# Layer 1's ConvFFN: seven block products for eight in the up-projection, and the down-projection as a stage of its own

## The chip, the core and the metric

The kernel runs on one core of a Trainium2 chip. The metric is the device time of one execution, in microseconds (us): before, 2966.02 as the median of three runs, which lie between 2965.62 and 2966.78.

## The reference

A backbone of two layers over 1024 latent tokens and 256 context tokens of width 1024, in float32. Layer 0 mixes tokens by latent attention and pooling, layer 1 by grouped-query attention; each layer ends with a ConvFFN on the modulated norm of the tokens, and the program with a norm. What this case touches is layer 1's second half and the final norm:

```python
def modulate(x, shift, scale):
    return rms_norm(x) * (1.0 + scale) + shift

def conv_ffn(h, w_up, conv_w, conv_b, w_down):
    a = h @ w_up                       # 1024 -> 2 x 2816
    g, u = a[..., :D_FF], a[..., D_FF:]
    # acc = conv_b + a convolution of width 3 over the tokens of g
    return (jax.nn.silu(acc) * u) @ w_down

xl = xl + ml[:, 2] * ol                # the attention's output
xl = xl + ml[:, 5] * conv_ffn(modulate(xl, ml[:, 3], ml[:, 4]), ...)
return rms_norm(xl, g_final)
```

## The kernel before, in words

Features lie on partitions and tokens along the free axis: a tile is 128 features x 512 tokens, and the 1024 latent tokens are two chunks (0 and 1). TensorE (PE) multiplies a 128x128 weight block with such a tile. To keep float32's accuracy each operand is split into a high and a low part (names in `h` and `l`), and `mm3` makes three matmuls of each product: high x high, high x low, low x high. A weight of 128x1024 is loaded by `wload` into one of two buffers `raw`; GpSimd (POOL, line 117) or ScalarE (ACT) makes the high part `wh`, and VectorE (DVE, line 111) subtracts it for the low part `wl`.

The 2816 features of the FFN are 22 tiles f. For each f of layer 1 `ffn` does the gate and the up-product of both chunks (4 x 24 matmuls: 8 blocks along the width of 1024, 3 matmuls each), the convolution (`conv`: ACT line 1645, DVE 1646 and 1647, ACT 1648) and the mix with u (`mix`: DVE 1656, ACT 1658, DVE 1659), which leaves the split activations `ah`, `al`. After every odd f, `product` adds the down-projection of two f's to the eight tiles of the stream x (2 x 8 x 6 matmuls, and 16 updates on DVE, line 1669).

`start1` writes the work around the FFN's beginning in the order in which each engine does it: the last out-projection's jobs (`out1`), with them the sum of squares and modulation of chunk 0 (`Norm`, `modulate1`), the first products of f = 0 on chunk 0, the norm of chunk 1, and then `n1.quick()`, the modulation of chunk 1's eight k-tiles (DVE lines 236, 249 and 251, POOL 238 and 239, a copy on ACT for each). `ahead(0)`, the gate of f = 1 on chunk 0, is what PE does meanwhile, and `gate(1, n1.QUICK)` takes chunk 1's k-tiles in the order in which they come.

Inside a region of `manual_schedule` the engines keep the code's order; code outside of one is put in order by a scheduler, each instruction where its engine is expected to be free. The FFN between `start1` and `finish1` is left to the scheduler. `finish1` is written out again: the tokens end in three pieces p, q and t (`Piece`: the last products, the update, squares, their sum over partitions on PE, the root by logarithm and exponential on ACT, lines 167 to 170, and the scaled output). ACT needs a table in its engine for these two functions; `tables` loads one ahead of its use (line 263).

## Time and profile before

| | before |
|---|---|
| runs, median of 3 | 2966.02 us |
| profiled execution, its span | 2965.5 us |
| PE busy | 2885.9 us (97%) |
| DVE busy | 1938.7 us (65%) |
| ACT busy | 1103.3 us (37%) |
| POOL busy | 741.1 us (25%) |
| matmuls | 15134 |
| layer 1's FFN begins (first gate product behind the out-projection) | 2208.84 us |
| its last full down-projection | 2914.64 us |

The profile covers one execution, from its first to its last instruction; what lies around the span is the half microsecond by which the runs' median is above it. A busy share is a mean over the whole program; what an engine means for the end is read from a stage: there one engine is busy all the time, or some wait ends last. The views used below are the windows (busy time of each engine in a stretch, the clock granted to PE, DMA), the chain of waits (followed back from the last instruction), groups of instructions by line, the timeline of single instructions, and the DMA issues.

### The profile page before, as it was taken

The page shows a single profiled execution, that of the slowest core. Times are in us where ns is not written, and L with a number is a line of the kernel's source. Part 1 is how long each engine was busy: PE and PEld are TensorE (multiplying, and loading weights), DVE is VectorE, ACT ScalarE, POOL GpSimd, SP SyncE. Part 2 cuts the span into 40 slices and gives each one's busy share as a digit, 9 for nine tenths or more (in the row PEclk, how much of TensorE's full clock was granted, in tenths as well). Part 3 has the DMA queues.
Part 4 walks back from the last instruction along what each step waited for, and adds up shares of the span by engine and source line. Part 5 has one row for each costly group of instructions (what it writes and reads, how often), then busy time and mean ns, then how long its engine had stood idle before and what let it go on. Part 6 is the DMA issues. An engine that isn't in the chain of part 4 may idle for free.

```text
span 2965.5 us, 39212 instructions
## 1 busy us (share of the span) xinstructions
PE 2885.9 (97%) x15134; PEld 2405.5 (81%) x15134; DVE 1938.7 (65%) x3268; ACT 1103.3 (37%) x2263; POOL 741.1 (25%) x858
## 2 busy tenths in 40 slices
...
GB/s 223 69 154 120 23 18 53 128 192 72 93 85 92 87 100 100 86 43 36 29 43 57 22 43 15 1 1 1 43 93 50 47 53 50 44 50 43 43 57 57
DMA packets 65971, 194.04 MB, mean 65 GB/s; under 512 B 8436, under 2 KB 13748, under 8 KB 65528
## 3 DMA queue, kind: packets, MB, share of 16 engines
...
q14 instruction: 68, 0.56, 0.1%
...
## 4 chain that ended last, share of the span: by engine, by line
PE 79%; DVE 11%; ACT 3%; issue 3%; POOL 2%; DMA 2%; SPq 0%; DVEq 0%; ACTq 0%; POOLq 0%
PE u L72 18%; PE g L72 18%; PE d L72 17%; PE b L72 6%; PE pv L1253 5%; PE T L1240 4%; PE S L1173 2%; PE S L1175 2%; PE S L1174 2%; PE qk L72 1%; PE T L72 1%; DVE h L249 1%; DVE mx L1196 1%; DVE y L236 1%; DVE wl L111 1%
## 5 line engine op out<-in xcount | busy, mean ns | idle before, releaser
L72 PE MATMUL g<-h,wh 128*128 128x512 f32 (+1 forms) x1760 | 507.0, 373 | 2.2 <-DVE h L249 2.2
L72 PE MATMUL u<-h,wh 128*128 128x512 f32 (+1 forms) x1760 | 505.3, 372 | 0.0
L117 POOL TENSOR_SCALAR wh<-raw 128x1024 fp32r<-128x1024 f32 x134 | 146.6, 1095 | 1086.3 <-PE d L72 428.9
L72 PEld LDWEIGHTS g<-h,wh 128*128 128x128 f32 x1760 | 319.2, 189 | 65.3 <-DVE h L249 3.8
L72 PEld LDWEIGHTS u<-h,wh 128*128 128x128 f32 x1760 | 319.2, 188 | 62.4
L1634 ACT COPY g<-g 128x512 f32<-128x512 f32 (+1 forms) x109 | 59.5, 546 | 788.5 <-PE g L72 788.5
L1669 DVE SCALAR_TENSOR_TENSOR x<-d,mod,x 128x512 f32<-128x512 f32 (+1 forms) x352 | 254.9, 735 | 147.6 <-PE d L72 146.9
L72 PE MATMUL g<-h,wl 128*128 128x512 f32 (+1 forms) x880 | 328.1, 373 | 2.5 <-DVE wl L111 2.5
L72 PE MATMUL u<-h,wl 128*128 128x512 f32 (+1 forms) x880 | 327.5, 372 | 0.2 <-DVE wl L111 0.2
L72 PE MATMUL d<-ah,wl 128*128 128x512 f32 (+1 forms) x832 | 308.3, 371 | 0.0
L72 PE MATMUL d<-al,wh 128*128 128x512 f32 (+1 forms) x832 | 307.7, 370 | 0.0
L72 PE MATMUL d<-ah,wh 128*128 128x512 f32 (+1 forms) x832 | 307.6, 370 | 0.0
L111 DVE TENSOR_TENSOR wl<-raw,wh 128x1024 fp32r<-128x1024 f32 x174 | 218.9, 1259 | 103.6 <-POOL wh L117 73.5
L1243 DVE TENSOR_TENSOR tl<-T,th 128x512 fp32r<-128x512 f32 x328 | 225.4, 687 | 46.7 <-ACT th L1242 41.6
L1253 PE MATMUL pv<-th,v 128*128 128x256 f32 x976 | 253.7, 309 | 1.4 <-ACT vo L1382 1.0
L1222 POOL TENSOR_SCALAR p<-p,sm 128x1280 f32<-128x1280 f32 x128 | 171.4, 1339 | 286.7 <-DVE sm L1221 194.3
L1196 DVE TENSOR_REDUCE mx<-S 128x1 f32<-128x512 f32 (+1 forms) x400 | 233.5, 584 | 10.9 <-PE S L1175 3.8
L1242 ACT CAST th<-T 128x512 fp32r<-128x512 f32 x328 | 192.3, 586 | 83.4 <-PE T L1240 75.2
L72 PE MATMUL b<-h,wh 128*128 128x512 f32 (+1 forms) x752 | 206.6, 362 | 4.6 <-DVE h L465 3.6
L1240 PE MATMUL T<-ident,p 128*128 128x128 f32 x1280 | 193.1, 272 | 1.5 <-POOL p L1222 1.5
L72 PEld LDWEIGHTS g<-h,wl 128*128 128x128 f32 x880 | 166.1, 189 | 33.8 <-DVE wl L111 3.0
L72 PEld LDWEIGHTS u<-h,wl 128*128 128x128 f32 x880 | 165.7, 188 | 31.7 <-DVE wl L111 0.6
...
## 6 DMA issues: line engine op xcount, KB each, us to landing
raw<-in_wup SPq DMA_DIRECT2D x88, 512.0 KB, 3.2
wm<-in_wmod SPq DMA_DIRECT2D x72, 512.0 KB, 3.6
raw<-in_wdn SPq DMA_DIRECT2D x44, 512.0 KB, 3.3
raw<-in_wout SPq DMA_DIRECT2D x32, 512.0 KB, 3.3
raw<-in_win SPq DMA_DIRECT2D x20, 512.0 KB, 3.8
wn<-in_wmodn SPq DMA_DIRECT2D x32, 256.0 KB, 5.3
xin<-in_xl SPq DMA_DIRECT2D x16, 256.0 KB, 6.0
wn<-in_wmodg SPq DMA_DIRECT2D x8, 512.0 KB, 3.9
```

What stands on the lines that cost most here:

```text
L72: PE.matmul(out, w, x, start=first and i == 0, stop=last and i == n - 1)
L111: eng.tensor_sub(lo[:, :n], raw[:, :n], f32(hi[:, :n]))
L117: P.tensor_scalar(out=hi[:, :n], in0=raw[:, :n], scalar1=1.0, scalar2=0.0, op0=ALU.mult, op1=ALU.add)
L1173: PE.matmul(o, qh, kh[:, ks], start=True, stop=False)
L1196: V.reduce_max(mx[:, j : j + 1], s, axis=AX.X)
L1222: P.tensor_scalar(out=self.p, in0=self.p, scalar1=sm[:, 3:4], scalar2=1.0, op0=ALU.mult, op1=ALU.mult)
L1240: PE.transpose(tb[:, (2 * j + i) * 128 : (2 * j + i) * 128 + 128], rows[i].p[:, c : c + 128], ident)
L1242: S.copy(hi, tb)
L1243: V.tensor_sub(lo, tb, f32(hi))
L1253: PE.matmul(out[0], st, mv, start=(u + j == 0 and x == 0), stop=(u + j == n - 1 and x == len(ops) - 1))
L1634: S.copy(g[:, G0[c] : G0[c] + n], b)
L1669: V.scalar_tensor_tensor(out=x, in0=b, scalar=mod[l, c // 2][:, 40 + d : 41 + d], in1=x, op0=ALU.mult, op1=ALU.add)
```

## The change

Four things change.

1. The up-projection of f = 1 to 21 is done as a product of 2x2 blocks: the width is cut in two halves of four k-tiles, the tokens in the two chunks, and the outputs in gate and up. In place of eight block products (of 12 matmuls each) there are seven (`strassen`, numbers 1 to 7), with sums and differences of the operands ahead and of the products behind. The weights' combinations are s1 to s4 (`wsum`, on POOL), a11 to a22 being the blocks themselves; each that is multiplied is split anew. The tokens' combinations t1 to t4 are made once, in the place of x (`Parts`). The products are added up in three PSUM banks x, y and z per f, and read by `u2`, `u3`, `c11`, `c12`, `c21` and `c22` of class `F`. f = 0 stays as it was.
2. The modulation is made in the place of x (`modulate_kept`), x itself having been stored in DRAM (`spill`) and being read back later.
3. The activations of each f are stored in DRAM (`store`), unsplit, and the down-projection follows as a stage of its own: `down(f)` loads weights and activations and splits both.
4. `finish1` becomes code behind that stage, with the same pieces in the same order; its `tables` call now follows code that is left to the scheduler.

```diff
+    def modulate_kept(k, x, r, m, first, dst, pool=True):
+        even = k % 2 == 0 or not pool
+        hi, lo = dst
+        sh = m[:, first * 8 + k : first * 8 + k + 1]
+        sc = m[:, first * 8 + 8 + k : first * 8 + 9 + k]
+        def scale():
+            if even:
+                V.scalar_tensor_tensor(out=x, in0=x, scalar=sc, in1=r, op0=ALU.mult, op1=ALU.mult)
+            else:
+                P.tensor_mul(x, x, r)
+                P.tensor_scalar(out=x, in0=x, scalar1=sc, scalar2=sh, op0=ALU.mult, op1=ALU.add)
+        def high():
+            if even:
+                S.activation(hi, x, AF.Identity, bias=sh)
+                S.activation(x, x, AF.Identity, bias=sh)
+            else:
+                S.copy(hi, x)
+        def low():
+            V.tensor_sub(lo, x, f32(hi))
+        return scale, high, low
...
+            if self.kept:
+                return modulate_kept(k, xs_of(self.c)[k], self.r, self.m, self.first, H[self.c][k], pool)
             return modulate1(k, xs_of(self.c)[k], self.r, self.n, self.m, self.first, tmp, H[self.c][k], pool, tag)
...
-        gate(0, range(6, 8))
-        load_ahead()
-        n1.total()
-        up(0, 1)
-        n1.root()
-        upper(0)
-        n1.rest()
-        up(1, 0)
-        load(1, 1)
-        n1.quick()
-        ahead(0)
-        gate(1, n1.QUICK)
-        mix(0)
-        upper(1)
-        down()
-        up(1, 1)
...
-    def finish1(gate, upper, conv, mix, down, product, spare):
-        regions.append(tc.manual_schedule(engines=ENGINES | {mybir.EngineType.SP}))
-        regions[-1].__enter__()
-        down()
...
-    ffn(1, (0, 1), (), start1, finish1)
+    d_act = tc.dram_tile([NF, 128, NLAT], F32, name="d_act")
...
+    def spill(d, c):
+        dma.dma_start(d_x[d][:, half_of(c)], xl[d][:, half_of(c)])
...
+    class Parts:
+        def __init__(self, j):
+            self.j = j
+            (self.b11, self.b12), (self.b21, self.b22) = [[xl[k][:, half_of(c)] for c in (0, 1)] for k in (j, j + 4)]
+        def first(self, e3, e1, e2):
+            e3.tensor_sub(self.b22, self.b22, self.b12)
+            e1.tensor_sub(self.b12, self.b12, self.b11)
+            e2.tensor_add(self.b11, self.b22, self.b11)
+        def fourth(self, eng):
+            eng.tensor_sub(self.b21, self.b21, self.b11)
...
+    def load_u(f, s):
+        rawu[f, s] = wpool.tile([128, 1024], F32, name="raw", tag="raw", bufs=2)
+        dma.dma_start(rawu[f, s], a["wup"][1, 2 * f + s])
...
+    SUMS = {"s1": ("a21", "a22", ALU.add), "s2": ("s1", "a11", ALU.subtract), "s3": ("a11", "a21", ALU.subtract), "s4": ("a12", "s2", ALU.subtract)}
+    def wsum(f, n, eng=P):
+        x, y, op = SUMS[n]
+        t = sums[f, n] = sp.tile([128, 512], F32, name="st", tag="st", bufs=3)
+        eng.tensor_tensor(out=t, in0=src_of(f, x), in1=src_of(f, y), op=op)
...
+    def wlow(f, n, eng=V):
+        hi, lo = A7[f, n]
+        eng.tensor_sub(lo, src_of(f, n), f32(hi))
...
+    PROD = {1: ("a11", "b11", "x"), 2: ("a12", "b21", "x"), 6: ("s2", "t2", "y"), 7: ("s3", "t3", "y"), 4: ("a22", "t4", "y"), 5: ("s1", "t1", "z"), 3: ("s4", "b22", "z")}
...
+    def strassen(f, i):
+        w, b, z = PROD[i]
+        if i in FIRST:
+            bank[f, z] = psb(z)
+        mm3(bank[f, z], [(wk(A7[f, w], j), operand_of(b, j)) for j in range(4)], first=i in FIRST, more=i not in FIRST)
...
+        def c22(self):
+            o = self.su[:, 512:1024]
+            V.tensor_add(o, bank[self.f, "z"], o)
+        def c12(self):
+            V.tensor_add(self.g_of(1), bank[self.f, "z"], self.u)
...
+        def store(self):
+            dma.dma_start(d_act[self.f], self.su[:, :1024])
...
+    b10 = plain(0, 1, 0, w0[1])
+    n1.rest()
+    for n in ("a11", "a12"):
+        whigh(1, n, P)
+    f0, f1 = F(0), F(1)
+    f0.open()
+    f1.open()
+    S.copy(f0.g_of(0), b00)
+    n1.quick()
+    wlow(1, "a11")
+    strassen(1, 1)
+    b01 = plain(0, 0, 1, w0[0], n1.QUICK)
+    wlow(1, "a12")
+    f1.s1()
...
+    for j, p in enumerate(parts):
+        p.first(P, V, V)
+        p.high(2, big() if j < 2 else small(spare[2 * j - 4]))
+        p.high(1, big() if j < 2 else small(spare[2 * j - 3]))
+        p.low(2)
+        p.low(1)
+    S.copy(f0.g_of(1), b01)
+    b11 = plain(0, 1, 1, w0[1])
+    strassen(1, 2)
...
+    def early(f):
+        me, old = fs[f], fs[f - 1]
+        nxt = f + 1 if f < NF - 1 else None
+        me.open()
+        strassen(f, 6)
+        old.c21()
+        whigh(f, "a22")
+        wlow(f, "a22")
+        if nxt:
+            load_u(nxt, 1)
+        old.conv(0)
+        strassen(f, 5)
+        me.u2()
+        old.conv2(0)
+        old.conv(1)
+        strassen(f, 2)
+        old.conv2(1)
+        old.silu(0)
+        old.mix(0)
+        if nxt:
+            whigh(nxt, "a11", P)
+        strassen(f, 7)
+        me.c11()
+        old.silu(1)
+        if nxt:
+            wlow(nxt, "a11")
+        old.mix(1)
+        old.store()
+    load_u(2, 0)
+    load_u(2, 1)
+    whigh(2, "a11", P)
+    wlow(2, "a11")
...
+    for f in range(1, NF):
+        nxt = f + 1 if f < NF - 1 else None
+        me, old = fs[f], fs[f - 1] if f > 1 else None
+        if f > 1:
+            early(f)
+        if nxt:
+            fs[nxt] = F(nxt)
+            strassen(nxt, 1)
+        me.u3()
+        me.c22()
+        if nxt:
+            wsum(nxt, "s1")
+            wsum(nxt, "s2")
+            whigh(nxt, "a12", P)
+            whigh(nxt, "s1")
+            whigh(nxt, "s2")
+        strassen(f, 3)
+        if nxt:
+            fs[nxt].s1()
+            wlow(nxt, "s2")
+            wlow(nxt, "s1")
+            wlow(nxt, "a12")
+            wsum(nxt, "s3")
+            whigh(nxt, "s3")
+        strassen(f, 4)
+        me.c12()
+        if nxt:
+            wlow(nxt, "s3")
+            wsum(nxt, "s4")
+            whigh(nxt, "s4")
+            wlow(nxt, "s4")
+            if nxt + 1 < NF:
+                load_u(nxt + 1, 0)
...
+    def down(f):
+        W[f] = wload(a["wdn"][1, f], p=dp if f % 4 > 1 else None, tag="dn" if f % 4 > 1 else "w")()
+        raw = wpool.tile([128, 1024], F32, name="raw", tag="raw", bufs=2)
+        dma.dma_start(raw, d_act[f])
+        acts[f] = {}
+        for c in (0, 1):
+            hi, lo = acts[f][c] = half("h"), half("h")
+            S.copy(hi, raw[:, half_of(c)])
+            V.tensor_sub(lo, raw[:, half_of(c)], f32(hi))
+    down(0)
+    down(1)
+    for f in range(0, NF - 2, 2):
+        down(f + 2)
+        down(f + 3)
+        for c in (0, 1) if f < NF - 4 else (0,):
+            for d in range(8):
+                product(c, d, 0, 512, (f, f + 1))()
+    regions.append(tc.manual_schedule(engines=ENGINES | {mybir.EngineType.SP}))
+    regions[-1].__enter__()
+    tables("natural_log_exp_and_others", False)
```

How this moves instructions is shown at three places, first the start of the FFN. On PE before, where the up-product of f = 0 ends; g is the gate of f = 1 on chunk 0 (`ahead`):

```order
L72 MATMUL u<-h,wh 128x512 x2
L72 MATMUL u<-h,wl 128x512
L72 MATMUL g<-h,wh 128x512 [waits Pool_49]
L72 MATMUL g<-h,wh 128x512
L72 MATMUL g<-h,wl 128x512 [waits DVE_49]
L72 MATMUL g<-h,wh 128x512 x2
L72 MATMUL g<-h,wl 128x512
L72 MATMUL g<-h,wh 128x512 x2
L72 MATMUL g<-h,wl 128x512
```

The same place on PE after; p is the plain product of f = 0, x the bank of block product 1 of f = 1, with the weight block a11:

```order
L72 MATMUL p<-h,wh 128x512 x2
L72 MATMUL p<-h,wl 128x512
L72 MATMUL x<-h,a11h 128x512 [waits Pool_49]
L72 MATMUL x<-h,a11h 128x512
L72 MATMUL x<-h,a11l 128x512 [waits DVE_49]
L72 MATMUL x<-h,a11h 128x512 x2
L72 MATMUL x<-h,a11l 128x512
L72 MATMUL x<-h,a11h 128x512 x2
L72 MATMUL x<-h,a11l 128x512
L72 MATMUL x<-h,a11h 128x512 x2
L72 MATMUL x<-h,a11l 128x512
L72 MATMUL p<-h,wh 128x512 [waits Activation_49]
```

24 matmuls on operands that only need a weight's low part have become 12, which wait for a11l. On DVE before, the end of chunk 1's modulation (lines 236 to 251) and what follows it:

```order
L236 SCALAR_TENSOR_TENSOR y<-x_6977,mod_66,r 128x512 [waits DVE_49]
L249 SCALAR_TENSOR_TENSOR h<-y,mod_66,h 128x512 [waits Activation_49]
L236 SCALAR_TENSOR_TENSOR y<-x_6979,mod_66,r 128x512 [waits DVE_49]
L249 SCALAR_TENSOR_TENSOR h<-y,mod_66,h 128x512 [waits Activation_49] x2
L251 TENSOR_TENSOR h<-z,h 128x512 [waits Activation_49]
L1646 SCALAR_TENSOR_TENSOR t_21647<-g,convw,t 128x512 [waits Activation_49]
L1647 SCALAR_TENSOR_TENSOR t<-g,convw,t_21647 128x512 [waits DVE_49]
L1656 TENSOR_TENSOR s<-t_21647,u 128x512 [waits PE_49,Activation_49]
L1659 TENSOR_TENSOR al<-s,ah 128x512 [waits Activation_49]
L111 TENSOR_TENSOR wl<-raw,wh 128x1024 [waits DMAHW3_49,Pool_49]
```

And after, where the modulation's low parts have line 277; x_6972 and the next are tiles of the stream, whose combinations (2471, 2472) and low parts (2486) come next:

```order
L264 SCALAR_TENSOR_TENSOR x_6979<-x_6979,mod_66,r 128x512 [waits DMAHW1_49]
L277 TENSOR_TENSOR h<-x_6977,h 128x512 [waits Activation_49]
L277 TENSOR_TENSOR h<-x_6979,h 128x512 [waits Activation_49]
L277 TENSOR_TENSOR h<-x_6975,h 128x512 [waits Activation_49]
L2524 TENSOR_TENSOR a11l<-raw,a11h 128x512 [waits DMAHW7_49]
L2524 TENSOR_TENSOR a12l<-raw,a12h 128x512
L2471 TENSOR_TENSOR x_6972<-x_6972 128x512 [waits Pool_49]
L2472 TENSOR_TENSOR x_6972<-x_6976,x_6972 128x512 [waits DVE_49]
L2486 TENSOR_TENSOR h<-x_6972,h 128x512 [waits Activation_49] x2
L2471 TENSOR_TENSOR x_6973<-x_6973 128x512 [waits Pool_49]
L2472 TENSOR_TENSOR x_6973<-x_6977,x_6973 128x512 [waits DVE_49]
```

The low part a11l, for which product 1 waits, stands behind the last of the modulation, and the convolution of f = 0 has moved behind the combinations.

The second place is the passage to the down-projection, which has none before. On PE after, in the last f: y takes block product 7 (weights s3), d is the first down product, z is product 3 (weights s4):

```order
L72 MATMUL y<-x_21787,s3h 128x512 x2
L72 MATMUL y<-x_21787,s3l 128x512
L72 MATMUL d<-h,wh 128x512 [waits Activation_49,Pool_49]
L72 MATMUL d<-h,wh 128x512 [waits DVE_49]
L72 MATMUL d<-h,wl 128x512
L72 MATMUL d<-h,wh 128x512 [waits Activation_49,Pool_49]
L72 MATMUL d<-h,wh 128x512 x2
L72 MATMUL d<-h,wl 128x512
L72 MATMUL d<-h,wh 128x512 [waits DVE_49]
L72 MATMUL d<-h,wl 128x512
L72 MATMUL d<-h,wh 128x512
L72 MATMUL z<-h,s4h 128x512 [waits DVE_49]
```

Six matmuls of the down-projection, which need the split weights and activations of f = 0 and 1, stand between block products 7 and 3 of the last f. What DVE does there, after; `h<-raw` at line 2815 is the low part of an activation read back, `su<-z` at 2568 is `c22`:

```order
L2583 SCALAR_TENSOR_TENSOR r<-g,convw,r 128x512 [waits Activation_49]
L2815 TENSOR_TENSOR h<-raw,h 128x512 [waits DMAHW4_49,Activation_49]
L2584 SCALAR_TENSOR_TENSOR r<-g,convw,r 128x512 [waits DVE_49]
L2815 TENSOR_TENSOR h<-raw,h 128x512 [waits Activation_49]
L111 TENSOR_TENSOR wl<-raw,wh 128x1024 [waits DMAHW5_49,Pool_49]
L2564 TENSOR_TENSOR su<-y,su 128x512 [waits DMAHW2_49,PE_49]
L2815 TENSOR_TENSOR h<-raw,h 128x512 [waits DMAHW6_49,Activation_49]
L2568 TENSOR_TENSOR su<-z,su 128x512 [waits DVE_49]
L2815 TENSOR_TENSOR h<-raw,h 128x512 [waits Activation_49]
L2829 SCALAR_TENSOR_TENSOR x_24940<-d,mod_66,x_24940 128x512 [waits DMAHW1_49,PE_49]
```

The weight low and the activations' lows of the down-projection stand among the convolution and the additions of the last f, two of them ahead of `c22` or just behind it.

The third place is on ACT. Before, the finish of the FFN: the table is loaded once, behind the last cast of the activations (the squares have line 2496):

```order
L1648 ACTIVATE t_25931<-t,convw 128x512 [waits DVE_49]
L1658 CAST ah<-s 128x512 [waits DVE_49]
L263 ACT_TABLE_LOAD
L2496 ACTIVATE x<-x_6972 128x512 [waits DVE_49]
L2496 ACTIVATE sq<-x_6973 128x512 [waits DVE_49,Pool_49]
L2496 ACTIVATE y<-x_6974 128x512 [waits DVE_49]
```

After, the first root of the finish; before these lines the same three activations stand without loads between them:

```order
L2862 ACTIVATE sq<-x_24942 128x256 [waits DVE_49,Activation_49]
L167 ACTIVATE x<-ss,epst 128x512 [waits PE_49]
L169 ACT_TABLE_LOAD
L169 ACTIVATE y<-x 128x512 [waits Activation_49]
L170 ACT_TABLE_LOAD
L170 ACTIVATE r<-y 128x512 [waits Activation_49]
L2862 ACTIVATE sq<-x_24934 128x256 [waits DVE_49]
```

And after, the start of the program, where before one load stands ahead of `scol`:

```order
L289 ACT_TABLE_LOAD x2
L514 ACT_TABLE_LOAD
L514 ACTIVATE scol<-scol 128x16 [waits DMAHW0_49]
L515 ACTIVATE srow<-srow 2x1024 [waits DMAHW1_49]
L289 ACT_TABLE_LOAD
```

A load now stands ahead of each logarithm (169) and each exponential (170) in the finish, in all three pieces, and the one of `tables` has moved to the start of the program.

## Rows read from the trace of the kernel before

**Rows 1.** Two lines of the profile's page: busy time of the engines, share of the span and instructions; and the DMA rate in the span's 40 equal slices.

```profile
PE 2885.9 (97%) x15134; PEld 2405.5 (81%) x15134; DVE 1938.7 (65%) x3268; ACT 1103.3 (37%) x2263; POOL 741.1 (25%) x858
...
GB/s 223 69 154 120 23 18 53 128 192 72 93 85 92 87 100 100 86 43 36 29 43 57 22 43 15 1 1 1 43 93 50 47 53 50 44 50 43 43 57 57
```

**Rows 2.** Windows: the stretch, its length, busy time and instructions of PE, PEld, DVE, ACT and POOL in it, the clock granted to PE, the DMA share and GB/s. The first is the start of layer 1's FFN, the second lies inside it, the last two are the finish.

```profile
2208.84:2256.84 48.00, 46.14 (x195) 36.11 (x195) 36.08 (x42) 19.97 (x30) 13.39 (x13) 1.00 0.23 77
2300.00:2850.00 550.00, 550.00 (x2370) 445.58 (x2369) 249.01 (x312) 89.11 (x134) 55.81 (x85) 1.00 0.14 48
2914.64:2949.40 34.76, 34.61 (x245) 32.10 (x243) 29.80 (x51) 20.07 (x38) 11.13 (x9) 1.00 0.15 54
2949.40:2965.50 16.10, 1.31 (x5) 0.64 (x3) 9.42 (x17) 6.04 (x15) 7.26 (x9) 0.57 0.43 147
```

**Rows 3.** Two links of the chain of waits in the steady FFN: start, duration, engine, output and line, instructions.

```profile
2256.84 22.29 PE d L72 x96
2279.13 11.16 PE g L72 x48
```

**Rows 4.** Timeline at the FFN's start: start, duration, engine, line, operation, out<-in, instructions. PE's first two matmuls behind the up-product of f = 0, then DVE's first and last step of chunk 1's modulation.

```profile
2220.92 0.63 PE L72 MATMUL g<-h,wh 128*128 128x512 f32 x2
...
2220.35 2.46 DVE L236 SCALAR_TENSOR_TENSOR y<-x,mod,r 128x512 f32<-128x512 f32 x2
...
2232.90 0.68 DVE L251 TENSOR_TENSOR h<-z,h 128x512 fp32r<-128x512 f32 x1
```

**Rows 5.** Timeline of DVE and POOL in chunk 0's modulation, and two of DVE's steps later; in brackets the idle time ahead and what ended it.

```profile
2192.08 0.75 DVE L1354 SCALAR_TENSOR_TENSOR x<-b,mod,x 128x512 f32<-128x512 f32 x1 [0.92 <-PE b L72]
2192.75 1.19 DVE L236 SCALAR_TENSOR_TENSOR hi<-x,mod,r 128x512 f32<-128x512 f32 x1
2193.86 2.31 DVE L111 TENSOR_TENSOR wl<-raw,wh 128x1024 fp32r<-128x1024 f32 x1
...
2205.91 0.69 DVE L251 TENSOR_TENSOR h<-z,h 128x512 fp32r<-128x512 f32 x1 [5.35 <-PE b L72]
2206.52 0.68 DVE L1483 TENSOR_TENSOR x<-x,y 128x512 f32<-128x512 f32 x1
...
2191.23 1.29 POOL L238 TENSOR_TENSOR z<-x,r 128x512 f32<-128x512 f32 x1 [3.03 <-DVE h L251]
...
2193.37 1.73 POOL L1483 TENSOR_TENSOR x<-x,y 128x512 f32<-128x512 f32 x1
...
2201.01 1.30 POOL L1483 TENSOR_TENSOR x<-x,y 128x512 f32<-128x512 f32 x1
...
2213.81 0.69 DVE L1496 TENSOR_TENSOR lo<-x,hi 128x512 fp32r<-128x512 f32 x1 [0.69 <-ACT hi L1495]
...
2223.85 0.75 DVE L236 SCALAR_TENSOR_TENSOR y<-x,mod,r 128x512 f32<-128x512 f32 x1
```

**Rows 6.** Groups of instructions by line and shape from 2256 to 2900 us: count | busy us, mean ns of one | idle time ahead and what ended most of it.

```profile
L1669 DVE SCALAR_TENSOR_TENSOR x<-d,mod,x 128x512 f32<-128x512 f32 x152 | 112.9, 749 | 77.5 <-PE d L72 76.9
L111 DVE TENSOR_TENSOR wl<-raw,wh 128x1024 fp32r<-128x1024 f32 x57 | 69.5, 1219 | 39.5 <-POOL wh L117 39.3
L117 POOL TENSOR_SCALAR wh<-raw 128x1024 fp32r<-128x1024 f32 x57 | 59.9, 1050 | 404.9 <-PE d L72 183.8 <-issue 153.6 <-DMA raw<-in_wdn 23.7
...
L1658 ACT CAST ah<-s 128x512 fp32r<-128x512 f32 x37 | 23.0, 621 | 98.5 <-DVE s L1656 98.5
...
L1570 POOL TENSOR_SCALAR h<-raw 128x512 fp32r<-128x512 f32 x4 | 2.4, 620 | 9.4 <-DMA raw<-in_wdn 9.4
```

**Rows 7.** DMA issues of the page: count, KB each, median us from issue to landing. The first are the down-projection's weights, the second modulation weights at the program's start.

```profile
raw<-in_wdn SPq DMA_DIRECT2D x44, 512.0 KB, 3.3
...
wn<-in_wmodn SPq DMA_DIRECT2D x32, 256.0 KB, 5.3
```

**Rows 8.** Windows of 2 us early in the program, columns as in rows 2: PE has little to do in the first two.

```profile
60.00:62.00 2.00, 0.66 (x3) 0.19 (x1) 1.69 (x4) 1.27 (x2) 0.00 (x0) 1.00 0.00 0
62.00:64.00 2.00, 0.63 (x2) 0.31 (x2) 1.32 (x3) 0.62 (x1) 0.00 (x0) 0.98 0.00 0
64.00:66.00 2.00, 1.94 (x4) 1.12 (x5) 2.00 (x6) 1.27 (x2) 0.07 (x1) 0.50 0.00 0
66.00:68.00 2.00, 2.00 (x7) 1.58 (x7) 1.97 (x5) 1.57 (x4) 2.00 (x2) 0.67 0.00 0
```

**Rows 9.** Timeline of ACT in the finish (the table load between a cast and the first square, then logarithm and exponential of the first root), and of PE at the program's start.

```profile
2915.47 0.62 ACT L1658 CAST ah<-s 128x512 fp32r<-128x512 f32 x1 [1.14 <-DVE s L1656]
2916.11 1.28 ACT L263 ACT_TABLE_LOAD   x1
2917.51 0.64 ACT L2496 ACTIVATE x<-x 128x512 f32<-128x512 f32 x1
...
2931.14 0.63 ACT L169 ACTIVATE y<-x 128x512 f32<-128x512 f32 x1
2931.81 0.63 ACT L170 ACTIVATE r<-y 128x512 f32<-128x512 f32 x1
...
4.23 9.53 PE L436 MATMUL mod<-wn,scol 128*2 128x512 f32 x16 [4.23 <-DMA wn<-in_wmodn]
18.88 0.80 PE L203 MATMUL ss<-hi,ones 128*128 128x512 f32 x1 [5.12 <-ACT hi L195]
```

588 lines of the change are left out of this document (366 added, 222 removed).

## The prediction

> **What bounds the kernel now.** I read the busy line first: TensorE (PE) works in 97% of the span [rows 1]. Then the stage around the change by windows: from 2300 to 2850 us PE is busy 550.00 of 550.00 us and does 2370 matmuls at a granted clock of 1.00, so one 128x512 matmul takes 550/2370 = 0.232 us, while VectorE (DVE) is busy 249, ScalarE (ACT) 89 and GpSimd (POOL) 56 [rows 2]. The chain of waits says the same: in this stage it holds only PE links, 22.29 us for 96 matmuls and 11.15 for 48 [rows 3]. So what counts is first the number of matmuls, then every place where PE must wait. Two such places lie in what the change touches: the start of the FFN (2208.84 to 2256.84, 195 matmuls worth 45.3 us in 48.0) and the tail after 2949.40, where PE has 5 matmuls left and the other engines end the program [rows 2].
>
> **What it removes.** Of the 22 feature tiles 21 need 84 matmuls for 96 in the up-projection: 21 x 12 = 252 matmuls x 0.232 = **58.5 us**. The number of matmuls of the down-projection is the same, and nothing ahead of layer 1's last out-projection moves on PE.
>
> **Start-up.** Before, the modulation of the second token half runs on DVE from 2220.35 to 2233.6 [rows 4], and PE covers it: it does 24 matmuls of f = 1 on the first half, and then takes the k-tiles one by one. The order now puts block product 1 of f = 1 there, 12 matmuls for 24, and they wait for the low part a11l, which stands on DVE behind the whole modulation. PE is done with the plain up-product at 2220.9 [rows 4] and then has nothing. The modulation takes 13.2 us in before; its in-place form has one more step on ACT for even k-tiles, I take 14.1: it ends at 2234.5, a11l follows, PE begins at about 2236. Bounds: 2232 and 2239.
>
> After that DVE sets the pace until block product 1 of f = 2. From a11l(1) to a11l(2) I count 42 DVE operations (a12l, four times two combinations and two lows, the lows of s1 to s4 and a22, four times one combination and two lows, four convolution steps, two mixes, one addition). Two-input operations follow each other every 2206.52 - 2205.91 = 0.61 us [rows 5]: 25.6 us. POOL has 8 sums or differences of 128x512 in this stretch, 1.29 us each, and they do not run beside DVE's: the sum at 2193.37 took 1.73 (alone 1.30, at 2201.01) and the low part at 2193.86 behind it 2.31 (1.22 on average [rows 6]), and the modulation step at 2192.75 took 1.19 for 0.75; the update at 2192.08, which reads PSUM, took its 0.75 in the middle of a POOL product [rows 5]. So I add them in full: 10.3. With 1.6 for ACT's casts (0.62 each [rows 6]) not covered, 37.5: product 1 of f = 2 begins at 2236 + 37.5 = 2273.5. In these 52.6 us from 2220.9 PE does 108 matmuls, 25.1 us; it stands still for 27.5. Before lost 48.0 - 192 x 0.232 = 3.4 around the same place, of it some 2.5 behind 2220.9. The extra loss is **25.0**. Bounds: 15, if POOL's sums fall into DVE's waits and the modulation is not longer (8 x 1.29 less), and 32, if ten more of the lows wait 0.69 for their cast, as the one at 2213.81 does [rows 5].
>
> The Trainium skill (SBUF — State Buffer, Who interferes with whom) says that a DVE instruction with two SBUF inputs and a GpSimd instruction that reads SBUF exclude each other for the whole instruction, and that a DVE instruction with at most one SBUF input does not contend. The rows above agree with both parts. Were it not so, the start-up would be shorter by the 10.3.
>
> **Steady stage, f = 2 to 21.** A period is 84 matmuls, 19.5 us. DVE per period: seven lows and four convolution steps on the shared port, 11 x 0.61 to 0.67 = 7.2, five operations that read PSUM at 0.67, 3.3. POOL: four sums and two mixes at 1.29, two 128x512 casts at 0.62 [rows 6], 9.0. Port together 16.2 of 19.5; ACT 11 operations of 0.6 to 0.7, 7.2. I walked the order through one period: the tightest place is c22, the addition out of bank z before product 3 may go on in it; it is ready 12.8 us after the period's first product, and needed at 13.9 (60 matmuls). All other parts come over 1.5 us early. I take **0**; the bounds are 0 and 6 (0.3 per period).
>
> **Handover to the down-projection.** In the last period the order has six matmuls of the first down product between block products 7 and 3. They need tokens and weights of f = 0 and 1, four 512 KB loads through the two buffers called raw. A load of this size lands in 3.3 us [rows 7]; each of the last two waits until the parts of the one before in its buffer are made, and those lows stand on DVE among the convolution. By this walk activations of f = 1 are split 16.0 us after the last period's first product, where PE arrives at 11.2 (48 matmuls), and c22, now behind their low part on DVE, ends at 18.05. [...] It ends at 24.8, for 18.1 without the wait: **6.7**. Bounds 1.5 (loads as early as their buffers, the lows in time) and 12 (5.3 us per load, as the 256 KB weight loads at the program's start take [rows 7]).
>
> **Down stage.** 912 matmuls up to the finish, 211.6 us, 22.3 for a pair of tiles. DVE per pair: 16 updates at 0.67, two 128x1024 lows at 1.22, four 128x512 lows at 0.61: 15.6. It also stands still where two weight lows are neighbours: both use the same raw buffer, so the second waits for a load (3.3) and POOL's cast (1.05 [rows 6]), 4.4, and about 1.5 more for an activation's load: 21.5 of 22.3. I take **0** with little to spare.
>
> **Finish.** The preload of ACT's table for logarithm and exponential stood at the finish in before: 1.28 us at 2916.11 [rows 9]. The order now has it at the start of the program, where it does nothing, and a load ahead of every logarithm and every exponential of the three roots. One root's two steps lie back to back now (2931.14, 2931.81 [rows 9]); each gets 1.28 longer, 2.6 a root. The last root is on the path that ends the program: 2.6. The first two delay DVE's outputs, which has 34.76 - 29.80 = 5.0 us free in this stage [rows 2]: of their 5.1 I take about half, 2.4. **5.0**, bounds 2.6 and 8. At the start two more loads (2.6) keep ACT from its first operation; PE then begins its first 16 matmuls later, but it ends them 5.1 us before it can go on at 18.88 [rows 9]: 0.
>
> The Trainium skill (ScalarE: Activation LUTs, What ACT_TABLE_LOAD costs) gives 1283 ns for a load and about 1380 ns for a drain with it. The load agrees; of a drain this trace shows nothing, since the cast before ends at 2916.09, the load begins at 2916.11, and the next operation follows 0.12 us after it. By the page the last root would cost 2.8 us more.
>
> The spills, stores and reloads (16 of 256 KB, 22 + 22 + 8 of 512 KB, 30 MB in some 700 us, 43 GB/s) lie beside this: the stage moves 48 GB/s with a DMA share of 0.14 [rows 2], and the program's first slice 223 [rows 1].
>
> **Sum**, against the profiled execution's 2965.5: 2965.5 - 58.5 + 25.0 + 6.7 + 5.0 = 2943.7. The median of the runs is 2966.0, 0.5 above: **2944**.
>
> **Rivals.**
> 1. *Smaller losses*, 0.14: start-up 15 to 18, handover 1.5, finish 2.6: 2966.0 - 58.5 + 17 + 1.5 + 2.6 = 2929. For it: DVE waits for ACT and POOL's sums may fit there. Against: the order puts the modulation in front in any case, so 15 us of waiting at 2220.9 are certain.
> 2. *DVE becomes the bound of the down stage*, 0.14: with 21.5 of 22.3 us used and two loads of 3.3 in DVE's way, it decides from a landing of 3.7 us on. At 5.3 they add 2.0 each, less 0.8 of slack: 3.2 a pair x 9 = 29: 2973, slower. At 4.5, 1.6 x 9 = 14: 2958. For it: the two neighbouring lows, and four loads where there were two. Against: the same loads land in 3.3 now.
> 3. *The shared port becomes the bound of the up stage*, 0.10: the gain is 2.8 us a period; with the 36.7 us of losses above it is used up when a period takes (58.5 - 36.7)/20 = 1.1 us more, 20.6. For it: DVE and POOL already have 16.2 of 19.5 on one port, and c22 has 1.1 to spare. At 21.4 us a period: 2944 + 38 = 2982, slower; at 20.1: 2956.
> 4. *A longer start-up*, 0.05: 40 us instead of 25, if the 42 operations go one by one with ACT: 2959.
> 5. *The matmuls do not become fewer*: 0.01, since the order counts 2824 of 128x512 for 3076 from the FFN on.
>
> **Chances.** Main case 0.56, its own range 2934 to 2953. A measurement of this kernel tells about 0.2%, 6 us, from no change: faster is below 2960, slower above 2972. Slower: a third of rival 2 and half of rival 3, and a little of the rest: 0.11. Between: 0.06. Faster: 0.83. The range for 8 in 10 takes in rival 1 and the milder half of rivals 2 to 4: 2928 to 2966.
>
> **What would show it.** The profile after should have PE idle from 2221 to about 2236 in one piece and some 12 us more in pieces up to 2273; periods of 19.5 us; one wait of 3 to 7 us before the first down product; six table loads in the finish. Wrong would be: periods over 20 us with PE waiting for DVE's c22, pairs over 22.5 us in the down stage with PE waiting for a weight's low part, or a start-up that ends before 2262 or after 2282.

## The result, and the profile after

The changed kernel takes 2943.15 us (median of four runs, 2939.58 to 2944.04) for 2966.40 before: a ratio of 0.9918, interval 0.9904 to 0.9932. Forecast were 2944 us, with a range of 2928 to 2966. The profiled execution has a span of 2942.3 us, 23.2 less than before; its own run took 2944.04, so 1.7 us lie around the span, and the half microsecond given for before is only the distance of the median.

The page of the changed kernel, the line that answers to the first of [rows 1], and the new loads of stored activations (the down-projection's weights land in 3.3 us as in [rows 7]):

```profile
PE 2835.1 (96%) x14882; PEld 2362.4 (80%) x14882; DVE 2069.0 (70%) x3462; ACT 1180.9 (40%) x2401; POOL 909.1 (31%) x986
...
raw<-d_act SPq DMA_DIRECT2D x22, 512.0 KB, 3.5
```

There are 252 matmuls fewer (15134 to 14882). Windows of the changed kernel, columns as in [rows 2]: the wait for a11l, the rest of the start-up, the steady up stage, the handover and the down stage:

```profile
2220.90:2236.00 15.10, 0.04 (x1) 0.04 (x1) 14.14 (x15) 8.06 (x13) 11.51 (x8) 0.58 0.00 0
2236.00:2273.50 37.50, 32.54 (x118) 25.50 (x119) 32.62 (x44) 17.13 (x29) 6.63 (x5) 0.85 0.30 98
2273.50:2640.00 366.50, 366.48 (x1573) 295.16 (x1573) 228.64 (x301) 127.26 (x207) 183.26 (x189) 1.00 0.23 81
2640.00:2675.50 35.50, 32.35 (x133) 25.69 (x132) 20.57 (x26) 10.76 (x18) 14.19 (x14) 0.95 0.43 148
2675.50:2880.00 204.50, 204.50 (x880) 165.26 (x880) 157.45 (x210) 23.77 (x41) 22.54 (x21) 1.00 0.32 106
```

PE is full in the two long stages; all the waiting lies in the first two windows, in the fourth and in the finish. PE's waits from 2215 us on are few enough to be listed, with the time in total, the times and the longest; the two for `ss` belong to the finish:

```profile
PE x L72 <- DVE a11l L2524: 15.5, 1, 15.5
PE ss L203 <- ACT hi L2869: 8.0, 2, 5.4
PE y L72 <- DVE x L2558: 5.0, 1, 5.0
PE d L72 <- POOL su L2592: 3.1, 1, 3.1
```

The last of these is put down to GpSimd's mix `su`, which ends at about the same moment as ACT's cast `h` of f = 1's activations. It is this cast that the product reads; in runs 1, 2, 3 and 8 the same wait is put down to it.

The timeline of the same places, PE first (product 1 of f = 1 where it goes on, the plain product behind it, product 7, product 3 behind product 1 of f = 2, the first down product, whose second tile waits, and the first matmul behind product 4 of the last f), then DVE around a11l and at the end of the start-up:

```profile
2235.96 0.80 PE L72 MATMUL x<-h,a11l 128*128 128x512 f32 x1 [15.53 <-DVE a11l L2524]
2240.40 0.64 PE L72 MATMUL p<-h,wh 128*128 128x512 f32 x2
2265.04 1.19 PE L72 MATMUL y<-h,s3h 128*128 128x512 f32 x2 [4.96 <-DVE x L2558]
2273.57 0.63 PE L72 MATMUL z<-h,s4h 128*128 128x512 f32 x2
2662.47 0.62 PE L72 MATMUL d<-h,wh 128*128 128x512 f32 x2
2666.49 1.11 PE L72 MATMUL d<-h,wh 128*128 128x512 f32 x3 [3.15 <-POOL su L2592]
2675.34 0.39 PE L72 MATMUL d<-h,wh 128*128 128x512 f32 x1
...
2218.67 2.44 DVE L264 SCALAR_TENSOR_TENSOR x<-x,mod,r 128x512 f32<-128x512 f32 x2
2231.36 2.89 DVE L277 TENSOR_TENSOR h<-x,h 128x512 fp32r<-128x512 f32 x2 [0.68 <-ACT x L272]
2234.16 1.75 DVE L2524 TENSOR_TENSOR a11l<-raw,a11h 128x512 fp32r<-128x512 f32 x1
2235.83 1.76 DVE L2524 TENSOR_TENSOR a12l<-raw,a12h 128x512 fp32r<-128x512 f32 x1
2237.51 1.77 DVE L2471 TENSOR_TENSOR x<-x 128x512 f32<-128x512 f32 x1
2239.32 1.65 DVE L2472 TENSOR_TENSOR x<-x,x 128x512 f32<-128x512 f32 x1
...
2253.20 0.69 DVE L2524 TENSOR_TENSOR s2l<-st,s2h 128x512 fp32r<-128x512 f32 x1 [0.23 <-ACT s2h L2518]
...
2270.40 0.68 DVE L2524 TENSOR_TENSOR a11l<-raw,a11h 128x512 fp32r<-128x512 f32 x1
```

PE stands 15.53 us for a11l, then 4.96 ahead of product 7 for u2 (line 2558, output x), and runs slowly behind each wait: the ten matmuls to 2240.40 take 4.44 us where 2.32 would do, the 24 from 2265.04 to 2273.57 take 8.53 for 5.57. That is 15.5 + 5.0 + 2.1 + 3.0 = 25.6. Before lost 2.3 there, with 145 matmuls in this window of before (columns as in [rows 2]):

```profile
2220.92:2256.84 35.92, 34.23 (x146) 27.02 (x145) 27.79 (x32) 15.54 (x23) 9.96 (x11) 1.00 0.22 74
```

The extra loss is 23.3.

GpSimd explains DVE's durations. Its rows in the stretch, four tokens' differences (line 2470) and the first three of the four sums of weights (2513):

```profile
2226.26 1.64 POOL L2470 TENSOR_TENSOR x<-x,x 128x512 f32<-128x512 f32 x1 [0.62 <-DVE h L277]
2230.76 4.60 POOL L2470 TENSOR_TENSOR x<-x,x 128x512 f32<-128x512 f32 x3 [2.87 <-DVE h L277]
2235.32 1.72 POOL L2513 TENSOR_TENSOR st<-raw 128x512 f32<-128x512 f32 x1
2237.12 1.61 POOL L2513 TENSOR_TENSOR st<-st,raw 128x512 f32<-128x512 f32 x1
2238.69 1.72 POOL L2513 TENSOR_TENSOR st<-raw 128x512 f32<-128x512 f32 x1
```

From 2234 to 2241 the two engines take turns, and each operation of DVE lasts 1.65 to 1.77 for 0.68. The last rows of after are ACT's in the finish, the start of the first and of the third root; they answer to [rows 9]:

```profile
2901.37 0.69 ACT L167 ACTIVATE x<-ss,epst 128x512 f32<-128x512 f32 x1 [0.88 <-PE ss L204]
2902.08 1.28 ACT L169 ACT_TABLE_LOAD   x1
2903.37 0.63 ACT L169 ACTIVATE y<-x 128x512 f32<-128x512 f32 x1
2904.02 1.28 ACT L170 ACT_TABLE_LOAD   x1
...
2929.70 0.47 ACT L167 ACTIVATE x<-ss,epst 128x256 f32<-128x256 f32 x1 [1.13 <-PE ss L204]
```

From the first root to the end it is 2942.3 - 2901.37 = 40.9 us. In before the same operation began just ahead of the logarithm in [rows 9], 35.1 us from the end:

```profile
2930.42 0.69 ACT L167 ACTIVATE x<-ss,epst 128x512 f32<-128x512 f32 x1 [0.87 <-PE ss L204]
```

### The profile page after: what moved, and what is told of

Read it like the earlier page. It is cut to its first block, busy times and chain, and to the rows that moved or that the text cites. A ratio compares the mean times of both kernels' runs of the same rounds, so it can differ in the third digit from the quotient of the medians.

```text
span 2942.3 us, 39629 instructions
## 1 busy us (share of the span) xinstructions
PE 2835.1 (96%) x14882; PEld 2362.4 (80%) x14882; DVE 2069.0 (70%) x3462; ACT 1180.9 (40%) x2401; POOL 909.1 (31%) x986
## 4 chain that ended last, share of the span: by engine, by line
PE 65%; DVE 13%; issue 9%; POOL 6%; ACT 4%; DMA 2%; SPq 0%; POOLq 0%; DVEq 0%; ACTq 0%
PE d L72 17%; PE g L72 10%; PE u L72 10%; PE b L72 6%; PE pv L1279 5%; PE T L1266 4%; PE S L1199 2%; PE S L1201 2%; PE S L1200 2%; POOL su L2592 2%; POOL st L2513 2%; PE qk L72 1%; DVE s2l L2524 1%; PE T L72 1%; DVE mx L1222 1%
## 5 line engine op out<-in xcount | busy, mean ns | idle before, releaser
L72 PE MATMUL g<-h,wh 128*128 128x512 f32 (+1 forms) x1056 | 286.0, 358 | 0.4 <-DVE h L249 0.4
L72 PE MATMUL u<-h,wh 128*128 128x512 f32 (+1 forms) x1056 | 284.6, 357 | 0.0
L72 PE MATMUL d<-h,wh 128*128 128x512 f32 (+1 forms) x768 | 224.5, 377 | 3.1 <-POOL su L2592 3.1
L72 PEld LDWEIGHTS g<-h,wh 128*128 128x128 f32 x1056 | 186.7, 189 | 31.7 <-DVE h L249 1.2
L72 PEld LDWEIGHTS u<-h,wh 128*128 128x128 f32 x1056 | 186.6, 188 | 31.5
L72 PE MATMUL g<-h,wl 128*128 128x512 f32 (+1 forms) x528 | 189.3, 359 | 2.5 <-DVE wl L111 2.5
L72 PE MATMUL u<-h,wl 128*128 128x512 f32 (+1 forms) x528 | 188.5, 357 | 0.0
L72 PE MATMUL d<-ah,wl 128*128 128x512 f32 (+1 forms) x528 | 188.3, 357 | 0.0
L1266 PEld LDWEIGHTS T<-ident,p 128*128 128x128 f32 x1280 | 156.6, 140 | 35.3 <-POOL p L1248 3.3
L1279 PE MATMUL pv<-tl,v 128*128 128x256 f32 x656 | 177.2, 281 | 0.0
```

The lines of the kernel that those rows point to most:

```text
L72: PE.matmul(out, w, x, start=first and i == 0, stop=last and i == n - 1, skip_group_check=more)
L1266: PE.transpose(tb[:, (2 * j + i) * 128 : (2 * j + i) * 128 + 128], rows[i].p[:, c : c + 128], ident)
L1279: PE.matmul(out[0], st, mv, start=(u + j == 0 and x == 0), stop=(u + j == n - 1 and x == len(ops) - 1))
```

## The experiments

Each run is compared with the kernel before on the same chip. The runs stand here by question: the start-up (1, 2, 7, 4, 8), the finish (3), the handover (5, 6), and all together (9, 10). The times of one kernel spread by up to 7 us, and the profiles show where: chunk 1's modulation begins between 2214.0 and 2219.0 us, and between 2214.9 and 2218.7 in the three of the unedited kernel alone. The edits leave the work ahead of it as it was, but for a11l in runs 1, 8, 9 and 10 and the table loads at the program's start in runs 3, 9 and 10. So beside the ratio I give the stretch from the first modulation step (DVE line 264, 266 in some runs) to the end of the span: in three profiles of the unedited changed kernel it is 723.6, 723.7 and 723.5 us.

| run | median us | ratio to before, interval | stretch us |
|---|---|---|---|
| changed kernel again | 2943.24 | 0.9923, 0.9908 to 0.9938 | 723.7 |
| 1 a11l first | 2940.93 | 0.9915, 0.9900 to 0.9929 | 721.9 |
| 2 lows on GpSimd | 2951.03 | 0.9950, 0.9936 to 0.9965 | 730.7 |
| 3 table pinned | 2935.99 | 0.9897, 0.9881 to 0.9914 | 717.7 |
| 4 t4 later | 2942.32 | 0.9916, 0.9902 to 0.9931 | 723.5 |
| 5 PE's order at the handover | 2946.65 | 0.9929, 0.9913 to 0.9946 | 725.7 |
| 6 handover written out | 2936.69 | 0.9898, 0.9883 to 0.9912 | 720.3 |
| 7 lows on GpSimd, behind | 2944.10 | 0.9921, 0.9906 to 0.9935 | 723.4 |
| 8 start-up, both edits | 2943.71 | 0.9931, 0.9916 to 0.9946 | 723.8 |
| 9 8, 6 and 3 together | 2935.47 | 0.9899, 0.9884 to 0.9914 | 716.1 |
| changed kernel, third time | 2941.27 | 0.9925, 0.9909 to 0.9942 | 723.5 |
| 10 9 and a third row | 2933.80 | 0.9893, 0.9875 to 0.9911 | 713.4 |

The interval of every run overlaps that of the changed kernel, so it is the stretch, of one profile each, that tells the runs apart, and it has two flaws. In runs 1, 8, 9 and 10 a11l stands just ahead of the first modulation step, and 0.5 us of it fall out of the stretch. And the handover differs where no edit touches it. From product 6 of the last f to the matmul behind its product 4 it takes 23.9 to 24.4 us in the three unedited profiles and in runs 1, 2 and 3, but 22.4 to 22.7 in runs 4, 7 and 8: there PE went on behind its wait of 3.1 to 3.4 us at a granted clock of 1.00, where the changed kernel has 0.58 behind 3.15 us (2666.49 to 2670.38).

So the start-up is best read by itself, from the root's last step (line 175, or 177) to product 6 of f = 3. It takes 80.8 to 81.4 us in the profiles that do not edit it, 80.1 in run 1, 88.2 in run 2, 82.6 in run 4, 82.4 in run 7, 83.4 in run 8, 83.3 in run 9 and 80.5 in run 10.

**The changed kernel again**, beside runs 1 to 3: 

> The changed kernel itself, again, as the measure for the runs beside it: 2943 us, between 2939 and 2945 as in its first runs. All theories expect the same here.

And a third time, beside runs 8 and 9: 

> The changed kernel itself beside the two runs before, as their measure: a ratio to the kernel before of 0.992, and 723.6 us from the start of chunk 1's modulation to the end.

Both came out so.

**1. a11l first.**

```diff
-    n1.quick()
     wlow(1, "a11")
+    n1.quick()
     strassen(1, 1)
```

> Edit: the low part a11l of f = 1 is made ahead of chunk 1's modulation on VectorE, not behind it; nothing else moves. TensorE then has block product 1 at once and need not stand still from 2220.9 to 2236.0. Theory A (VectorE's chain of operations sets the pace of the start-up): the wait there goes (the first product begins at about 2222 us), but the plain products that follow chase the modulation's k-tiles, block product 6 still begins at about 2254 to 2255 and product 7 at about 2265, since s2l and the tokens' combinations come no earlier; the time is that of the changed kernel, 2943, within 3 us either way. Theory B (the loss is the 15 us for which TensorE waits for a11l): the whole start-up moves forward by 12 to 15 us, and the time is 2928 to 2932.

The 15.5 us wait is gone, and the stretch is 1.7 us shorter (1.2 with the 0.5 of a11l), not 12 to 15. What PE waits for now:

```profile
PE y L72 <- ACT s2h L2518: 8.4, 1, 8.4
PE y L72 <- DVE x L2558: 4.0, 1, 4.0
PE p L72 <- DVE h L277: 4.0, 5, 0.9
```

Of 20.5 us of waiting 16.4 are left, at product 6 above all. Product 6 begins 33.4 us after the first modulation step (35.5 to 35.9 in the unedited kernel). Theory A holds: a11l's place is why PE waits there, but the chain of the other engines sets the length of the start-up.

**2. Four lows on GpSimd.**

```diff
-        p.low(1)
+        p.low(1, P)
```

> Edit: the four low parts of t1 are made by GpSimd, which is idle from 2240.4 to 2254.6 us in the changed kernel, and no longer by VectorE. Theory A (a GpSimd operation and a VectorE operation with two inputs from SBUF exclude each other): the four cost 1.3 us each on the shared path in place of 0.61, so VectorE's operations beside them take longer, s2l comes 1 to 3 us later, and the time is 0 to 3 us above the changed kernel's 2943. Theory B (the engines run beside each other): VectorE's chain gets 4 x 0.61 = 2.4 us shorter and the time falls to about 2940.5; VectorE's operations keep their 0.6 to 0.7 us beside GpSimd's.

Neither: 7 us longer. The lows wait for ACT, and behind them in GpSimd's queue wait the sums that DVE needs. As a test of the two engines the run is spoiled, but it shows the matter elsewhere, since GpSimd is now idle from 2228 to 2239.7. DVE's rows there, from the modulation's last lows on:

```profile
2231.40 1.29 DVE L277 TENSOR_TENSOR h<-x,h 128x512 fp32r<-128x512 f32 x2 [0.67 <-ACT x L272]
2232.61 0.68 DVE L2524 TENSOR_TENSOR a11l<-raw,a11h 128x512 fp32r<-128x512 f32 x1
2233.21 0.69 DVE L2524 TENSOR_TENSOR a12l<-raw,a12h 128x512 fp32r<-128x512 f32 x1
2233.81 0.68 DVE L2471 TENSOR_TENSOR x<-x 128x512 f32<-128x512 f32 x1
2234.53 0.69 DVE L2472 TENSOR_TENSOR x<-x,x 128x512 f32<-128x512 f32 x1
```

The same six operations, from 2231.40 to 2235.22, take 3.8 us; beside GpSimd's they took from 2231.36 to 2240.97, 9.6 us.

**7. The same, behind the sums.**

```diff
-        p.low(1)
...
     wsum(1, "s3")
+    for p in parts:
+        p.low(1, P)
```

> Edit: as in the run that moved the four low parts of t1 to GpSimd, but they stand there behind the sum s3, so no sum waits for them (in the first form they were written among the sums, and GpSimd's own order held those up). Theory A (the two engines exclude each other on two-input operations): the stretch from a11l to s2l on VectorE, 19.0 us in the changed kernel, has four operations of 0.61 less and four of GpSimd's of 1.29 in it, of which up to 0.69 each fall into VectorE's waits for casts: it lasts 19 to 22 us, GpSimd's or VectorE's operations there last longer than alone, and the time is 2943 to 2946. Theory B (they run beside each other): 16.6 us for the stretch, VectorE's operations at 0.6 to 0.7 throughout, and 2940 to 2941.

From a11l (2230.66) to s2l (2251.14) 20.5 us for 19.0, in theory A's 19 to 22, as the time is in its 2943 to 2946. Three times the pair stands like this, a DVE operation of 0.69 at 1.80 beside GpSimd's 1.30; theory B has no place for it:

```profile
2238.76 1.80 DVE L2471 TENSOR_TENSOR x<-x 128x512 f32<-128x512 f32 x1
...
2238.71 1.30 POOL L2486 TENSOR_TENSOR h<-x,h 128x512 fp32r<-128x512 f32 x1 [1.80 <-ACT h L2479]
```

**4. Work for later products later.**

```diff
-        p.fourth(V)
-        p.high(4, pairs[1])
         p.low(3)
-        p.low(4)
...
+        if f == 1:
+            late()
```

`late` holds t4's parts, then the convolution, mix and store of f = 0.

> Edit: the parts of t4 (six of VectorE's operations), the convolution and mix of f = 0 (six more) are moved behind the addition u2, the low parts a11l of f = 2, s4l and a22l, and the additions u3 and c22 of f = 1; nothing is left out. Theory A (the order of VectorE's chain is what TensorE waits for ahead of block product 7, as u2 stands behind work that is needed only later): the wait of 5.0 us at product 7 goes and with it the half clock behind it (3.0 us for 24 matmuls); later waits of up to 2 us at products 3 and 4; the time is 6 to 8 us under the changed kernel's 2943, 2935 to 2937. Theory B (VectorE has too much work in the stretch, in whatever order): the wait moves on to product 3, 4 or to product 6 of f = 2, and the time stays within 2 us of 2943.

The wait at product 7 shrinks to 0.6 us, and product 3 begins 47.5 us after the first modulation step in place of 54.9. But product 6 of f = 2 now waits 4.0 us for s2h, and the stretch is 723.5. The row of PE, and ACT's rows ahead of s2h:

```profile
2273.41 1.22 PE L72 MATMUL y<-h,s2h 128*128 128x512 f32 x2 [3.98 <-ACT s2h L2518]
...
2271.61 0.72 ACT L2587 ACTIVATE r<-r,convw 128x512 f32<-128x512 f32 x1 [0.41 <-DVE r L2584]
...
2272.74 0.61 ACT L2518 CAST s2h<-st 128x512 fp32r<-128x512 f32 x1
```

The order did what theory A says at product 7; the total is theory B's. The start-up by itself is even 1.6 us longer (82.6 for 81.0); the shorter handover hides it in the stretch.

**8. Both start-up edits, and f = 0's convolution behind s2h.**

```diff
-            fs[nxt].s1()
+            if f > 1:
+                fs[nxt].s1()
             wlow(nxt, "s2")
             wlow(nxt, "s1")
+            if f == 1:
+                late_conv()
+                fs[nxt].s1()
```

> Edit: the start-up with both earlier edits (a11l ahead of the modulation; t4's parts behind u3 and c22) and with the convolution of f = 0 placed behind ScalarE's casts s1h and s2h and VectorE's s2l and s1l of f = 2, ahead of s1's copy. Theory A (the wait that moved on to block product 6 of f = 2 came from the order in ScalarE's queue, where f = 0's activations stood ahead of s2h): product 6 of f = 2 begins some 3 to 4 us earlier, measured from the start of the modulation, and the stretch from there to the end of the program is 4 to 6 us shorter than the changed kernel's 723.6. Theory B (VectorE's work as such is too much up to there): the wait moves on to products 5 or 2 of f = 2 and the stretch is within 2 us of 723.6.

723.8: theory B. Product 6 of f = 2 does begin earlier, by 6.4 us, but the wait is now 4.2 us at product 2 of f = 2, where the copy s1 writes a row that the activations of f = 0 leave only when they are stored; ACT's row:

```profile
2282.40 0.58 ACT L2554 COPY su<-x 128x512 f32<-128x512 f32 x1 [3.68 <-DMA d_act<-su]
```

Run 10 takes that away too.

**3. The table load pinned.**

```diff
-    tables("natural_log_exp_and_others", False)
+    tables("natural_log_exp_and_others", True)
```

> Edit: the load of the table for logarithm and exponential is pinned behind ScalarE's last work of the down stage, so one load stands at the finish, as in the kernel before, and the six loads ahead of the logarithms and exponentials go; the other engines' orders are unchanged. Theory A (the six loads lengthen the tail by the 5.0 us forecast; the traces' shift is 5.8): the time falls by 5 to 6 us to about 2937, and the first root's steps follow each other at 0.65 us again. Theory B (only the last root counts, as the first two are hidden): it falls by 2.6 us to about 2940.5. Theory C (the tail is longer for another reason, such as the order of the last pieces): no change.

The stretch is 5.9 us shorter, and from the first root to the end it is 34.8 us for 40.9. Theory A, and somewhat more than forecast. The roots follow each other without loads again; the three intervals, root to root and to the end, shrink from 14.2, 14.1 and 12.6 us to 11.6, 13.1 and 10.0:

```profile
2901.95 0.69 ACT L167 ACTIVATE x<-ss,epst 128x512 f32<-128x512 f32 x1 [0.90 <-PE ss L204]
2913.59 0.45 ACT L167 ACTIVATE x<-ss,epst 128x256 f32<-128x256 f32 x1
2926.69 0.47 ACT L167 ACTIVATE x<-ss,epst 128x256 f32<-128x256 f32 x1 [1.13 <-PE ss L204]
```

**5. PE's order alone at the handover.**

```diff
+                if pin and i == 0:
+                    tc.keep_in_program_order(ins)
```

`pin` is set for the first down product.

> Edit: on TensorE alone the six matmuls of the first down product stand behind block product 4 of the last f, as the code has them, in place of between products 7 and 3; VectorE's order ahead of c22 is kept, with c22 behind the first low part of f = 1's activations. Theory A (the handover's loss of about 6 us comes from the loads: c22 stands behind that low part, so product 3 waits as long): no gain, 2943 within 1.5 us, TensorE's wait of some 4 to 5 us now ahead of product 3. Theory B (the loss comes from where TensorE's six matmuls stand): the wait goes, 2938 to 2939.

No gain; theory A's wait, but worse than its band of 1.5 us: 2.0 us in the stretch, and 2946.65 at the median. PE's wait is now 5.3 us ahead of product 3, for `su`, the output of c22:

```profile
PE z L72 <- DVE su L2570: 5.3, 1, 5.3
```

**6. The handover written out.**

```diff
+        if not nxt:
+            split_a(0)
+            low1.append(wload(a["wdn"][1, 1])(later=True))
+            load_a(1)
         old.mix(0)
...
         me.u3()
         me.c22()
+        if not nxt:
+            W[1] = low1[0]()
+            split_a(1)
```

> Edit: the handover is written out in the last period: on TensorE as in the run before (the first down product behind block product 4), on VectorE u3 and c22 ahead of the weight low and the activations' lows of f = 1. Theory A (each of the two orders alone keeps product 3 waiting for the loads, both together free it): product 3 begins about 1.3 us after product 7, the loads of f = 1 land while products 3 and 4 run, and of the 5.9 us lost at the handover 3.5 to 5 come back: 2938 to 2939.5. Theory B (the loads are late for the down products in any order): the wait stands ahead of the first down product and nothing is gained, 2943.

The stretch is 3.3 us shorter, just under the 3.5 to 5 of theory A; PE waits 1.6 us ahead of product 3, and nothing ahead of the down products, which begin at 2668.77 right behind product 4. Theory A all the same; with run 5 it shows that the loads of f = 1 were in the way of c22 through DVE's order, and late for nothing else.

**9. All together.** The edit is that of runs 8, 6 and 3. 

> Edit: the start-up of the run before, the handover written out in the last period, and the pinned table load, together. If the three losses are separate, their gains add up: 6 us from the table, 3.5 from the handover and what the run before shows at the start-up (0 to 6): 10 to 15 us under the changed kernel, a ratio to the kernel before of 0.987 to 0.989. If they hide each other, less than 9 in all.

7.5 us in the stretch, less than 9, but not because the gains hide each other. By stages (7.0 in all with the 0.5 of a11l) the finish is 6.2 us shorter, 34.7 for 40.9, and the handover loses 1.9 for 5.0, as in runs 3 and 6; the start-up is 2.3 longer, 83.3 for 81.0, as in run 8, whose own shorter handover hid that. The losses of finish and handover are separate; that of the start-up came back in no order tried so far but for the 0.9 us of run 1.

**10. A third row.**

```diff
-            self.su, self.t = row(1, name="su"), {}
+            self.su, self.t = (np_.tile([128, 1024], F32, name="su3", tag="su3") if f == 2 else row(1, name="su")), {}
```

> Edit: all three edits as in the run before, and the row su of f = 2 has a buffer of its own, so that the copy s1 of f = 2 no longer waits until the activations of f = 0 are stored; the copy and the low part a12l stand ahead of f = 0's convolution. Theory A (what was left of the start-up's gain was eaten by that store: 4.2 us of wait at product 2 and 2 to 3 us of half clock behind it): from the start of chunk 1's modulation to the end 716.1 becomes 710 to 712, a ratio to the kernel before of 0.987 to 0.9885. Theory B (VectorE's work in the stretch is the bound, and the wait moves on once more, to product 7 or 3 of f = 2): 715 to 717.

713.4, between the two: the wait at product 2 is gone, and 2.1 us come back at product 7 of f = 2. This is the fastest kernel of the study, 2933.80 us at the median; its interval overlaps those of runs 3, 6 and 9, so the ratios do not settle how much of it comes from the start-up. The profile says 80.5 us for the 81.0 of the changed kernel: nearly all of the gain is from finish and handover.

## Why the prediction was right, step by step

The mechanism, the places and the sum were right: 2944 for 2943.15. The terms, from the traces:

| term | forecast | measured | how |
|---|---|---|---|
| matmuls | -58.5 | -58.5 | 252 fewer, at before's 0.232 |
| start-up | +25.0 | +23.3 | waits and half clock above, less before's 2.3 |
| steady up stage | 0 | +1.8 | 2273.57 to 2662.47, 388.9 us for 1668 matmuls |
| handover | +6.7 | +5.0 | 2662.47 to 2675.34, 12.87 us, less 34 matmuls |
| finish | +5.0 | +5.8 | 40.9 for 35.1 us; run 3: 5.9 |

They add up to -22.6. From the end of chunk 1's root (2219.21 in before, where the low part wl takes DVE before the modulation) the stretch fell from 746.3 to 723.6, 22.7.

**Start-up.** PE went on in product 1 at 2235.96 as forecast (2236), in part by luck: the modulation took 15.6 us for the 14.1 forecast, but began at 2218.67 for before's 2220.35, since wl no longer stands ahead of it (1.0 us of the 1.7). The second half was shorter: a11l of f = 2 ended at 2271.1 for 2273.5. The sizes inside were off and nearly cancelled. I put all eight of GpSimd's operations behind a11l, 10.3 us; four ran beside the modulation already, the last of them into a11l, and the four sums of weights that were left lengthened DVE's operations by some 4.2. The 42 operations took some 27.7 us for 25.6, and the waits for ACT's casts 3.3 for 1.6. The split of the loss was off as well: 12 us more of standing were forecast behind 2236, and it was 5.0, with 5.1 of half clock that I had in no term. Nor did DVE set the pace to the end: product 1 of f = 2 began at 2270.30 without a wait, and it was the half clock behind the wait for u2 that put its end at 2273.57. The loss of 3.4 that I gave before counts 192 matmuls where [rows 2] has 195 (2.7); behind 2220.92 it was 2.3 for the 2.5 put down. So the mechanism held, and that 25.0 came within 2 us is partly luck. That GpSimd and DVE exclude each other, on which the sum rested, is shown by runs 2 and 7. Runs 1, 4 and 8 show that none of the orders tried there was alone to blame.

**Steady stage.** Rival 3 did not come: a period is 19.57 us, and PE is busy 366.48 of 366.50. The walk held: in the period from 2299.01 c22 is ready 12.8 us after the first product and needed at 13.9. The chain of waits does not say so by itself. It runs through GpSimd and DVE there, one period of it reading like this (start, duration, engine):

```profile
2363.67 1.76 POOL su L2592
...
2372.17 1.70 DVE s2l L2524
...
2376.31 6.89 issue
2383.24 1.77 POOL su L2592
```

More than half of this chain is `issue`, time in which nothing is seen to wait; whether PE waited is decided by the windows. The 1.8 us over 0 is a matmul's mean of 0.2332 for 0.2321. Where that comes from was not tried.

**Handover.** The term was too large by 1.7 us, and half of that is a misreading: between products 7 and 3 of the last f stand not six matmuls of the down-projection but ten, the six of the first down product and four of the second. The order's own lines show ten, and the trace has 34 matmuls from 2662.47 to 2675.34, of which products 3 and 4 are 24. So the time without a wait is 82 matmuls, 19.0 us, for the 18.1 of the walk. The other half is that the period ended at 24.0 for 24.8: the first activations of f = 1 were split 15.8 us after its first product (16.0 forecast), and c22 ended at 16.4 for 18.05. PE waited 3.15 us for the cast of these activations, and not for c22, which was there before product 3 came to its turn at 17.8. Of the 24.8, 6.8 lie behind c22, and 24 matmuls are 5.6 of them; no run shows the other 1.2, and in its place the trace has 1.6 of slow clock ahead of and in product 3, ten matmuls from 2666.49 to 2670.38 in 3.89 us for 2.32. Runs 5 and 6 confirm the step by which c22 stood behind that low part: with the down product moved away, PE waits for c22 itself.

**Down stage.** Rival 2 did not come either: PE is busy 204.50 of 204.50. The loads landed in 3.3 and 3.5 us, under the 3.7 from which it decides, and DVE was busy 157.45 of 204.5, 17.2 a pair for the 15.6 put down.

**Finish.** The term was mis-sized on the low side: I let half of the first two roots' 5.1 us be hidden, and run 3 shows 2.6, 1.0 and 2.6 for the three roots, the first one in full. The loads are 1.28 us, and the next operation begins 0.01 to 0.02 us behind them. The Trainium skill (ScalarE: Activation LUTs, What ACT_TABLE_LOAD costs) adds a drain of about 1380 ns to each load; no trace here shows it, and by an estimate from that page's figures the tail would have grown by about twice as much.
